# Weight sums of the gate/up quads: accumulating transfers for all of them, and five quads a block instead of four

## The chip, the core and the metric

The kernel runs on one core of a Trainium2 chip. A core has TensorE (PE: matrix products, with a separate weight load, PEld), VectorE (DVE), ScalarE (ACT), GpSimd (POOL) and SyncE (SP), each with an instruction queue of its own that it works off strictly in order, and sixteen DMA engines that serve the transfers of all queues. SyncE issues nearly all loads here; GpSimd issues the transfers that add what they bring to what already lies in on-chip memory (SBUF). The metric is the device time in microseconds (us), the median of several runs.

## The reference

A block of a language model for 256 tokens of width 2048, in float32: a gated feed-forward, a mixer, and a second feed-forward.

```python
def _swiglu(x, w_gate, w_up, w_down):
    return (jax.nn.silu(x @ w_gate) * (x @ w_up)) @ w_down

f = _swiglu(_rmsnorm(h, ln_ffn1_pre[l]), ffn1_gate[l], ffn1_up[l], ffn1_down[l])
h = h + MACARON_WEIGHT * _rmsnorm(f, ln_ffn1_post[l])
mx = _hybrid_mixer(_rmsnorm(h, ln_mix_pre[l]), w_in[l], ...)
h = h + _rmsnorm(mx, ln_mix_post[l])
f = _swiglu(_rmsnorm(h, ln_ffn2_pre[l]), ffn2_gate[l], ffn2_up[l], ffn2_down[l])
h = h + MACARON_WEIGHT * _rmsnorm(f, ln_ffn2_post[l])
```

w_gate and w_up are 2048 x 5632, w_down is 5632 x 2048. The mixer isn't touched by the change.

## The kernel before, in words

Tokens are two halves of 128 rows (h = 0, 1). Every float32 operand is split into a high part (a cast on ScalarE, `wH<-w`) and a low remainder (a subtraction on VectorE, `wL<-w,wH`), and each product is three matmuls (`mm3`): high by high, high by low, low by high. Weights come as tiles of 128 rows by 512 columns (256 KB); two of them side by side fill one buffer of 128x1024, and one split handles both.

**Stages.** The first feed-forward's gate/up part takes from the start to about 440 us, its down part to about 685 us, the mixer to about 1300 us, and the second feed-forward the rest. The gate/up part has eleven blocks of 512 gate columns (`f`) and 512 up columns (`l`). A block runs over 16 row tiles of the weights (k = 0 to 15), with four sums in PSUM: f0, f1, l0, l1, one per column group and token half.

**Pairs and quads.** An ordinary step (`pair`, L902) loads the two tiles of rows k and k+1 for one column group and multiplies both by both token halves. A *quad* (`Columns`, L874) takes a 2 x 2 set of tiles, rows k and k+1 by gate and up, and forms the eight products with seven, after Strassen and Winograd. So each quad saves one product of three matmuls, and pays with sums of weight tiles and sums of token tiles (`sums`, L706). With g(k) and u(k) for the gate and up tile of row k, the sums of weights are t1 = u(k) + g(k), t3 = g(k+1) + g(k), t2 = u(k) + t3 and t4 = u(k+1) + t2.

A gate/up quad has two steps. `early` (L928) runs during the block ahead: it loads the four tiles, makes the sums, splits u(k), t2, t1 and t3 and does four of the seven products. `late` (L947) runs in the block itself: it loads g(k+1) and u(k+1) once more, splits them and t4, and does the other three. `block_seq` (L1016) mixes the late steps and pairs of one block with the early steps of the next.

**How the sums are made before.** `four` (L908) has two ways. In most quads VectorE adds: t1 and t3 in one instruction of 128x1024, t2 and t4 in one of 128x512 each (L932, L936). In the quads of index 3 (`GATE_ACC`, L56) SyncE loads g(k) twice into the buffer of t1 and t3, and GpSimd issues two transfers with `accum_op=ALU.add` (L925), which add u(k) and g(k+1) from memory onto them. `GATE1` and `GATE2` (L49) give the number of quads in each of the eleven blocks. The down part has ten quads for each half of its columns (`quad`, L972), two of them (`DOWN_ACC`, L55) with accumulating transfers.

**What sets the order.** The operations aren't issued as the code writes them: `Plan.simulate` (L312) lets a small model of the engines run, with durations (`cost`, L231), a transfer rate (`RATE`), a landing time and an extra for accumulating transfers (`ADDING`), deadlines and buffer counts, and writes down each engine's queue in the order in which the model issued (`emit`, L503, where L525 issues every instruction; that is why the profile shows L525 everywhere). On the chip every queue keeps that order, whatever lands late. Buffers: five of 128x1024 for loaded weights (`w32`), five each for `wH` and `wL`, and 36 units of 128x1024 for all else. `KEPT` (L116) says how many of the eleven results of the gate/up part are split at once and written out for later sums; the others are kept unsplit until the down part needs them, and the down part's quads begin after them.

Of the kernel before, what the change touches and what calls it, by code (L numbers as in the profile page):

```python
# [12 lines left out]
F32 = mybir.dt.float32  # L13
# [34 lines left out]
EASE = 2.0  # L48
GATE1 = [0, 0, 3, 4, 4, 4, 4, 4, 4, 4, 4]  # L49
GATE2 = [0, 0, 3, 4, 4, 4, 4, 4, 4, 4, 4]  # L50
# [54 lines left out]
CARRY = 1200.0  # L105
ADDING = 3000.0
SWITCH = 100.0
# [7 lines left out]
LEND = 11  # L115
KEPT = 4  # L116
IN_ORDER = ("w32", "wH", "wL")


class Plan:  # L120
# [110 lines left out]
    def cost(s, o, name, w, r, k):  # L231
# [642 lines left out]
class Columns:  # L874

    def __init__(s, blk, wf, cf, wl, cl, at, KT, sm, quads, bank, apart=None):
        s.b, s.wf, s.cf, s.wl, s.cl, s.at, s.KT, s.sm = blk, wf, cf, wl, cl, at, KT, sm
        s.dma = ()
        s.quads, s.new, s.apart = quads, bank, apart
# [27 lines left out]

    def four(s, k):  # L908
        q = s.b
        t13 = q.unit((P, 2, 512), F32, "t13")  # L910
        if k not in s.dma:
            va, vb = q.raw4(k, s.wf, s.cf, s.wl, s.cl)
            q.nc.vector.tensor_tensor(out=t13, in0=va,
                                      in1=vb[:, :1].to_broadcast([P, 2, 512]), op=ALU.add)
            return va, vb, t13
        get = lambda k, f: (s.wf if f else s.wl)[k * P:k * P + P,
                                                 (s.cf if f else s.cl):][:, :512]
        for i in range(2):
            q.nc.sync.dma_start(out=t13[:, i], in_=get(k, 1))
        va, vb = [q.raw().rearrange("p (a c) -> p a c", a=2) for _ in range(2)]  # L920
        q.nc.sync.dma_start(out=va[:, 0], in_=get(k, 0))
        q.nc.sync.dma_start(out=va[:, 1], in_=get(k + 1, 1))
        q.nc.sync.dma_start(out=vb[:, 1], in_=get(k + 1, 0))
        for i in range(2):
            q.nc.gpsimd.dma_start(out=t13[:, i], in_=get(k + i, i), accum_op=ALU.add)  # L925
        return va, vb, t13
# [45 lines left out]
    def quad(s, k):  # L972
        q = s.b
        V = q.nc.vector
        va, vb, t13 = s.four(k)
        b11, b22 = q.halves(va)
        V.tensor_tensor(out=vb[:, 0], in0=va[:, 0], in1=t13[:, 1], op=ALU.add)
        t4 = q.tmp("t4")
        V.tensor_tensor(out=t4, in0=vb[:, 1], in1=vb[:, 0], op=ALU.add)
        t1, t3 = q.halves(t13)  # L980
        t2, b21 = q.halves(vb)
        h4 = q.unit((P, 2, 512), F32R, "h4")
        q.split(t4, h4[:, 0], h4[:, 1])
# [30 lines left out]
class Kernel(Block):  # L1014
# [30 lines left out]

    def ffn(s, wg, wu, wd, uT, rs, gpost, resid, emit, reload, quads, downs, xs=None):
        nc = s.nc
# [38 lines left out]
        for b in range(1, nb):  # L1086
            jobs[b] = Columns(s, wg, b * 512, wu, b * 512, s.T_at(nT) if b > 1 else at, NKD,
                              su, [2 * i for i in range(quads[b])],
                              s.psum if b % 2 else s.bank)
            jobs[b].dma = [2 * i for i in GATE_ACC if i < quads[b]]  # L1090
        for b in range(1, nb):
# [12 lines left out]
        s.down(wd, late_T, NKF, s.post(gpost, 0.5, resid, emit, reload, xs is None), raws,  # L1104
               downs, 4 * KEPT, DOWN_ACC)

# [30 lines left out]
    def down(s, wd, at, KT, ev, raws, plan, q0=0, acc=()):  # L1137
        sm = {}
        for c, (nq, first, step) in ((0, plan[0]), (2, plan[1])):
            J = Columns(s, wd, c * 512, wd, c * 512 + 512, at, KT, sm,  # L1140
                        [q0 + 2 * i for i in range(nq)], s.bank, s.psum)
            quads = list(J.quads)
            J.dma = [quads[i] for i in acc if i < nq]
            tail = J.rest[-min(TRAIL, KT - 2 * nq) // 2:] if c else []
# [863 lines left out]
def kernel(tc, x, ln_ffn1_pre, ln_ffn1_post, ffn1_gate, ffn1_up, ffn1_down,  # L2008
# [11 lines left out]
    with ExitStack() as ctx:  # L2020
# [10 lines left out]
        def at_tok(u):  # L2031
            return lambda h, c: u[h][c // 2][:, (c % 2) * 512:(c % 2) * 512 + 512]
# [68 lines left out]
        def emit1(h, c, ap):  # L2101
# [3 lines left out]
              at_tok(xr), emit1, load_to(xr, lambda h: x[0, h * P:h * P + P]),  # L2105
              GATE1, DOWN1, (load, turn, squares, finish, scaled))
        uT3, rs3, pre3, _ = s.next_pre(lambda: s.col["ln_ffn2_pre"])
# [9 lines left out]
        def emit(h, c, ap, queue=nc.sync):  # L2117
            queue.dma_start(out=out[0, h * P:h * P + P, c * 512:c * 512 + 512], in_=ap)
        s.ffn(ffn2_gate[0], ffn2_up[0], ffn2_down[0], uT3, rs3, ln_ffn2_post[0],
              at_tok(h2), emit, load_to(h2, lambda h: hsp[1, h]), GATE2, DOWN2)  # L2120
        s.plan.emit()
# [49 lines left out]
```

## Time and profile before

| | |
|---|---|
| time, median of 3 runs | 1985.75 us (1985.63 to 1986.48) |
| the profiled execution: its time | 1987.15 us |
| its span, first to last instruction | 1985.4 us |
| granted TensorE clock | 0.999 |
| busy PE, DVE, ACT, POOL | 1974.6, 1813.0, 1210.7, 118.8 us |
| moved by DMA | 503.19 MB, mean 253 GB/s |

A row of the profile's groups names the line, the engine, the operation, what it writes and reads, the shape, the count, then busy us and mean ns of one, and the idle time of the engine just before them with what ended it. Numbers are left off the names of buffers, so `w` is any buffer of loaded weights and `t` any unit for sums. A view by stretches gives each engine's busy time in a piece of the span and the share of the sixteen DMA engines. The view of the DMA queues gives for each queue packets, MB, and the time of its packets as a share of the time of sixteen engines: q1 is SyncE's queue, q0 GpSimd's. Matmuls overlap in the rows (389 ns each), so their pace is read from the time between them.

### The profile page before, as it was taken

The page shows a single profiled execution, that of the slowest core. Times are in us where ns is not written, and L with a number is a line of the kernel's source. Part 1 is how long each engine was busy: PE and PEld are TensorE (multiplying, and loading weights), DVE is VectorE, ACT ScalarE, POOL GpSimd, SP SyncE. Part 2 cuts the span into 40 slices and gives each one's busy share as a digit, 9 for nine tenths or more (in the row PEclk, how much of TensorE's full clock was granted, in tenths as well). Part 3 has the DMA queues.
Part 4 walks back from the last instruction along what each step waited for, and adds up shares of the span by engine and source line. Part 5 has one row for each costly group of instructions (what it writes and reads, how often), then busy time and mean ns, then how long its engine had stood idle before and what let it go on. Part 6 is the DMA issues. An engine that isn't in the chain of part 4 may idle for free.

```text
span 1985.4 us, 28410 instructions
## 1 busy us (share of the span) xinstructions
PE 1974.6 (99%) x9692; PEld 1630.8 (82%) x9692; DVE 1813.0 (91%) x2303; ACT 1210.7 (61%) x1552; POOL 118.8 (6%) x190
## 2 busy tenths in 40 slices
PE   9999999999999999999999999999999999999998
PEld 7888888888888888888888788888888888888886
DVE  7999999989998988998899779998999999899986
ACT  8566656666655767864665455665556556666553
POOL 0000000000001020001400100010000000000000
PEclk9999999999999999999999999999999999999999
DMA  9988899887768888757666498777898999777684
GB/s 319 323 266 283 276 317 312 278 257 228 242 198 274 261 259 277 216 167 252 178 194 190 128 322 262 240 258 241 273 307 293 317 287 286 255 230 236 204 287 144
DMA packets 278000, 503.19 MB, mean 253 GB/s; under 512 B 25056, under 2 KB 53472, under 8 KB 277856
## 3 DMA queue, kind: packets, MB, share of 16 engines
q1 hardware_dynamic: 267280, 478.96, 73.6%
q0 software_dynamic: 10144, 22.03, 5.3%
q8 instruction: 76, 1.25, 0.2%
q14 instruction: 68, 0.56, 0.1%
q10 hardware_dynamic: 432, 0.40, 0.1%
HBM read 473.11 MB, written 27.13 MB: 252 GB/s over the span
## 4 chain that ended last, share of the span: by engine, by line
PE 94%; DVE 3%; DMA 1%; ACT 1%; issue 1%; SPq 0%; POOLq 0%; ACTq 0%; DVEq 0%
PE l L525 33%; PE f L525 30%; PE mm L525 22%; PE p L525 6%; DVE wL L525 1%; DMA w<-in_ffn_gate_dram 1%; PE pY L525 0%; PE pA L525 0%; ACT wH L525 0%; PE tr L525 0%; PE pU L525 0%; DMA w<-in_ffn_down_dram 0%; DVE AR L525 0%; DMA w<-in_w_in_dram 0%; PE pSa L525 0%
## 5 line engine op out<-in xcount | busy, mean ns | idle before, releaser
L525 ACT CAST wH<-w 128x1024 fp32r<-128x1024 f32 (+1 forms) x712 | 727.4, 1042 | 508.4 <-PE f L525 105.1
L525 DVE TENSOR_TENSOR wL<-w,wH 128x1024 fp32r<-128x1024 f32 (+1 forms) x712 | 848.8, 1209 | 92.8 <-ACT wH L525 68.8
L525 PE MATMUL l<-wL,xH 128*128 128x512 f32 x828 | 322.3, 389 | 0.0
L525 PE MATMUL l<-wH,xL 128*128 128x512 f32 x828 | 322.2, 389 | 0.0
L525 PE MATMUL l<-wH,xH 128*128 128x512 f32 x828 | 322.1, 389 | 0.0
L525 PE MATMUL f<-wH,xH 128*128 128x512 f32 x608 | 236.6, 389 | 0.0
L525 PE MATMUL f<-wH,xL 128*128 128x512 f32 x608 | 236.6, 389 | 0.0
L525 PE MATMUL f<-wL,xH 128*128 128x512 f32 x608 | 236.5, 389 | 0.0
L525 PE MATMUL mm<-wL,xH 128*128 128x512 f32 (+1 forms) x568 | 220.2, 388 | 1.1 <-DVE wL L525 1.1
L525 PE MATMUL mm<-wH,xH 128*128 128x512 f32 (+1 forms) x568 | 220.8, 389 | 0.5 <-ACT xH L525 0.5
L525 PE MATMUL mm<-wH,xL 128*128 128x512 f32 (+1 forms) x568 | 219.1, 386 | 0.0
L525 ACT CAST wH<-t 128x1024 fp32r<-128x1024 f32 (+1 forms) x158 | 165.3, 1046 | 81.6 <-PE f L525 32.3
L525 DVE TENSOR_TENSOR wL<-t,wH 128x1024 fp32r<-128x1024 f32 (+1 forms) x158 | 191.5, 1212 | 17.0 <-ACT wH L525 7.9
L525 PEld LDWEIGHTS l<-wL,xH 128*128 128x128 f32 x828 | 155.4, 188 | 32.4 <-DVE wL L525 0.2
L525 PEld LDWEIGHTS l<-wH,xH 128*128 128x128 f32 x828 | 155.4, 188 | 32.3
L525 PEld LDWEIGHTS l<-wH,xL 128*128 128x128 f32 x828 | 155.4, 188 | 32.2
L525 DVE TENSOR_TENSOR t<-w,w 128x1024 f32<-128x1024 f32 (+1 forms) x170 | 167.2, 988 | 7.5 <-DMA w<-in_ffn_down_dram 5.6
L525 PEld LDWEIGHTS f<-wL,xH 128*128 128x128 f32 x608 | 114.1, 188 | 23.7
L525 PEld LDWEIGHTS f<-wH,xL 128*128 128x128 f32 x608 | 114.1, 188 | 23.7
L525 PEld LDWEIGHTS f<-wH,xH 128*128 128x128 f32 x608 | 114.1, 188 | 23.6
L525 PEld LDWEIGHTS mm<-wL,xH 128*128 128x128 f32 x568 | 106.8, 188 | 22.7 <-DVE wL L525 2.3
L525 PEld LDWEIGHTS mm<-wH,xH 128*128 128x128 f32 x568 | 106.7, 188 | 22.5 <-ACT xH L525 0.9
(320 smaller groups left out, 2861.3 us busy)
## 6 DMA issues: line engine op xcount, KB each, us to landing
w<-in_w_in_dram SPq DMA_DIRECT2D x120, 512.0 KB, 4.5
w<-in_ffn_up_dram SPq DMA_DIRECT2D x106, 512.0 KB, 5.1
w<-in_ffn_up_dram SPq DMA_DIRECT2D x210, 256.0 KB, 5.1
w<-in_ffn_gate_dram SPq DMA_DIRECT2D x102, 512.0 KB, 6.0
w<-in_ffn_gate_dram SPq DMA_DIRECT2D x202, 256.0 KB, 5.0
w<-in_ffn_down_dram SPq DMA_DIRECT2D x96, 512.0 KB, 4.8
w<-in_ffn_down_dram SPq DMA_DIRECT2D x152, 256.0 KB, 4.1
cx<-T SPq DMA_DIRECT2D x33, 512.0 KB, 3.8
```

The lines of the kernel that those rows point to most:

```text
L525: ins = o.fn(*[real(x) for x in o.a], **{n: real(x) for n, x in o.k.items()})
```

## The change

Each gate/up quad now has a *mode* (`GMODE1`: 3, 3, 3, 1, 1 for the five quads of a block). In mode 1, VectorE makes t1, t3 and t2 as before; t4 begins as a copy of t2 by ScalarE, onto which a transfer from GpSimd's queue adds u(k+1). In mode 3, moreover, two transfers add u(k) and g(k) onto the loaded g(k) and g(k+1), which makes t1 and t3 in place; VectorE then makes t2 alone. Mode 3 takes its second buffer from the units instead of the weight ring. Counted from 0, blocks 2 to 9 have five quads and block 10 has four, where block 2 had three and blocks 3 to 10 four; blocks 0 and 1 have none. The down part's quads all go by VectorE (`DMODE1` is zero). The planner's extra for an accumulating transfer falls from 3000 to 800 ns, and `KEPT` from 4 to 2.

```diff
-GATE1 = [0, 0, 3, 4, 4, 4, 4, 4, 4, 4, 4]
+GATE1 = [0, 0, 5, 5, 5, 5, 5, 5, 5, 5, 4]
...
-DOWN_ACC = 6, 8
-GATE_ACC = 3,
+GMODE1 = [[3, 3, 3, 1, 1]] * 11
+GMODE2 = GMODE1
+DMODE1 = [0] * 10, [0] * 10
...
-ADDING = 3000.0
+ADDING = 800.0
...
-KEPT = 4
+KEPT = 2
...
+            if "accum_op" in k:
+                o.pace = 1000.0
...
+    def load(s, out, k, f):
+        s.b.nc.sync.dma_start(out=out, in_=s.at_w(k, f))
+
+    def plus_w(s, out, k, f):
+        s.b.nc.gpsimd.dma_start(out=out, in_=s.at_w(k, f), accum_op=ALU.add)
...
     def early(s, k):
-        va, vb, t13 = s.four(k)
-        V.tensor_tensor(out=va[:, 1], in0=va[:, 0], in1=t13[:, 1], op=ALU.add)
...
+        mode = s.mode(i)
+        va, vb = [q.raw(mode & 2).rearrange("p (a c) -> p a c", a=2) for _ in range(2)]
+        s.load(va[:, 0], k, 0)
+        s.load(vb[:, 0], k, 1)
+        s.load(va[:, 1], k + 1, 1)
...
-        V.tensor_tensor(out=s.t4[i - i % 2][:, i % 2], in0=vb[:, 1], in1=va[:, 1],
-                        op=ALU.add)
-        b11, t2 = q.halves(va)
-        t1, t3 = q.halves(t13)
+        t4 = s.t4[i - i % 2][:, i % 2]
+        if mode & 2:
+            s.plus_w(vb[:, 0], k, 0)
+            s.plus_w(va[:, 1], k, 1)
+            t2 = vb[:, 1]
+            add(t2, va[:, 0], va[:, 1])
+        else:
+            if not mode & 1:
+                s.load(vb[:, 1], k + 1, 0)
+            t13 = q.unit((P, 2, 512), F32, "t13")
+            add(t13, va, vb[:, :1].to_broadcast([P, 2, 512]))
+            t2 = va[:, 1]
+            add(t2, va[:, 0], t13[:, 1])
+        if mode & 1:
+            q.nc.scalar.copy(t4, t2)
+            s.plus_w(t4, k + 1, 0)
```

**GpSimd's queue, first feed-forward.** Before, in the middle of the gate/up part (`t` is the buffer of t1 and t3, two rows a block):

```order
L525 DMA t_359_1403<-in_ffn_gate_dram 128x512
L525 DMA t_359_1403<-in_ffn_up_dram 128x512
L525 DMA t_441_1798<-in_ffn_gate_dram 128x512
L525 DMA t_441_1798<-in_ffn_up_dram 128x512
L525 DMA t_521_2133<-in_ffn_gate_dram 128x512
L525 DMA t_521_2133<-in_ffn_up_dram 128x512
```

These six rows stand for three blocks. Now, from one block's early steps (`w` are the buffers of loaded tiles in mode 3, `t` those of t4):

```order
L529 DMA w_404_1596<-in_ffn_gate_dram 128x512
L529 DMA w_405_1603<-in_ffn_up_dram 128x512
L529 DMA t_350_1593<-in_ffn_up_dram 128x512
L529 DMA t_406_1740<-in_ffn_up_dram 128x512
L529 DMA w_423_1672<-in_ffn_gate_dram 128x512
L529 DMA w_424_1680<-in_ffn_up_dram 128x512
L529 DMA w_432_1714<-in_ffn_gate_dram 128x512
L529 DMA w_433_1721<-in_ffn_up_dram 128x512
L529 DMA t_380_1833<-in_ffn_up_dram 128x512
L529 DMA t_406_1740<-in_ffn_up_dram 128x512
L529 DMA t_434_1943<-in_ffn_up_dram 128x512 x2
```

Three quads of mode 3 stand there with two rows each, and between them the transfers onto t4; in one queue they wait for loads, for ScalarE's copies and for each other's turn.

**SyncE's queue, the same places.** Before, a quad with accumulation (t_521) and one without (w_507, w_508):

```order
L525 DMA t_521_2133<-in_ffn_gate_dram 128x512
L525 DMA w_501_2141<-in_ffn_gate_dram 128x512
L525 DMA w_501_2141<-in_ffn_up_dram 128x512
L525 DMA w_507_2155<-in_ffn_up_dram 128x512
L525 DMA w_507_2155<-in_ffn_gate_dram 128x512
L525 DMA t_521_2133<-in_ffn_gate_dram 128x512
L525 DMA w_508_2175<-in_ffn_gate_dram 128x512
L525 DMA w_508_2175<-in_ffn_up_dram 128x512
```

Now, two quads of mode 3 (w_404 with w_405, w_423 with w_424) and one of mode 1 (w_378 with w_379); x<-cx brings back a block's result, turned:

```order
L529 DMA w_404_1596<-in_ffn_gate_dram 128x512
L529 DMA w_405_1603<-in_ffn_gate_dram 128x512
L529 DMA w_404_1596<-in_ffn_up_dram 128x512
L529 DMA w_375_1621<-in_ffn_gate_dram 128x2x512
L529 DMA x_315_1638<-cx_89 32x4x256 x4
L529 DMA w_378_1661<-in_ffn_up_dram 128x512
L529 DMA w_378_1661<-in_ffn_gate_dram 128x512
L529 DMA w_423_1672<-in_ffn_gate_dram 128x512
L529 DMA w_424_1680<-in_ffn_gate_dram 128x512
L529 DMA w_423_1672<-in_ffn_up_dram 128x512
L529 DMA w_379_1706<-in_ffn_gate_dram 128x512
```

Every quad has three loads in its early step now, where it had four or five; the rest of what it needs has moved to the queue above.

More of the change, by code (lines that the diff above doesn't have):

```diff
@@ L906, in pair, with at_w @@
                 s.mul(f"{b}{h}", s.rows(i, h), (wH, wL))
[L908 to L926, printed above, removed]
+    def at_w(s, k, f):
+        w, c = (s.wf, s.cf) if f else (s.wl, s.cl)
+        return w[k * P:k * P + P, c:c + 512]
+    def load(s, out, k, f):
+        s.b.nc.sync.dma_start(out=out, in_=s.at_w(k, f))
+    def plus_w(s, out, k, f):
+        s.b.nc.gpsimd.dma_start(out=out, in_=s.at_w(k, f), accum_op=ALU.add)
     def early(s, k):
@@ L974, in quad @@
         V = q.nc.vector
-        va, vb, t13 = s.four(k)
+        add = lambda o, x, y: V.tensor_tensor(out=o, in0=x, in1=y, op=ALU.add)
+        mode = s.mode(s.quads.index(k))
+        va, vb = [q.raw(x).rearrange("p (a c) -> p a c", a=2) for x in (False, mode & 1)]
+        t13 = q.unit((P, 2, 512), F32, "t13")
+        t4 = vb[:, 0] if mode & 1 else q.tmp("t4")
+        if mode & 2:
+            s.load(t13[:, 0], k, 1)
+            s.load(t13[:, 1], k, 1)
+        s.load(va[:, 0], k, 0)
+        if not mode & 2:
+            s.load(vb[:, 0], k, 1)
+        s.load(va[:, 1], k + 1, 1)
+        s.load(vb[:, 1], k + 1, 0)
+        if mode & 2:
+            for i in range(2):
+                s.plus_w(t13[:, i], k + i, i)
+        else:
+            add(t13, va, vb[:, :1].to_broadcast([P, 2, 512]))
         b11, b22 = q.halves(va)
-        V.tensor_tensor(out=vb[:, 0], in0=va[:, 0], in1=t13[:, 1], op=ALU.add)
-        t4 = q.tmp("t4")
-        V.tensor_tensor(out=t4, in0=vb[:, 1], in1=vb[:, 0], op=ALU.add)
+        add(vb[:, 0], va[:, 0], t13[:, 1])
+        if not mode & 1:
+            add(t4, vb[:, 1], vb[:, 0])
         t1, t3 = q.halves(t13)
         t2, b21 = q.halves(vb)
+        if mode & 1:
+            s.plus_w(t4, k + 1, 0)
         h4 = q.unit((P, 2, 512), F32R, "h4")
@@ L1089, in ffn @@
                               s.psum if b % 2 else s.bank)
-            jobs[b].dma = [2 * i for i in GATE_ACC if i < quads[b]]
+            jobs[b].mode = lambda i, b=b: modes[b][i]
         for b in range(1, nb):
@@ L1142, in down @@
             quads = list(J.quads)
[L1143 removed]
+            J.mode = lambda i, c=c: acc[c // 2][i] if acc else 0
             tail = J.rest[-min(TRAIL, KT - 2 * nq) // 2:] if c else []
```

26 lines of the change are left out of this document (20 added, 6 removed).

## The prediction

> **What bounds the kernel now.** I read the page first: engine shares, then the chain that ended last.
>
> ```profile
> span 1985.4 us, 28410 instructions
> PE 1974.6 (99%) x9692; PEld 1630.8 (82%) x9692; DVE 1813.0 (91%) x2303; ACT 1210.7 (61%) x1552; POOL 118.8 (6%) x190
> ...
> PE 94%; DVE 3%; DMA 1%; ACT 1%; issue 1%; SPq 0%; POOLq 0%; ACTq 0%; DVEq 0%
> ```
>
> TensorE (PE) is busy 99% of the span and is 94% of the chain; DMA is 1% of it. Then the chain in order of time, inside the first feed-forward's gate/up stage. Its columns are start, length, engine and group.
>
> ```profile
> 176.78 11.56 PE l L525 x51
> ...
> 217.58 11.56 PE l L525 x51
> ...
> 258.38 11.56 PE l L525 x51
> ```
>
> The same run of 51 matmuls returns every 40.80 us: that is one block of 512 gate and 512 up columns. One matmul costs 11.56 / 51 = 0.2267 us; a block has 16 x 2 x 2 x 3 = 192, less 3 for each of four quads, 180, and 180 x 0.2267 = 40.8 us. So PE runs without a hole, and nothing but fewer matmuls can shorten it as long as its food arrives. Who brings the food is the next view: busy time by stretches (PE, PEld, DVE, ACT, POOL, then granted clock, DMA share of 16 engines, GB/s). The first two are the stretches in which quads are made.
>
> ```profile
> 53.00:435.00 382.00, 382.00 (x1686) 316.28 (x1686) 363.95 (x383) 232.19 (x255) 14.94 (x19) 1.00 0.89 289
> 1342.00:1723.00 381.00, 381.00 (x1682) 315.48 (x1682) 355.98 (x369) 228.79 (x250) 13.97 (x16) 1.00 0.88 286
> 272.00:312.00 40.00, 40.00 (x178) 33.10 (x178) 38.46 (x41) 23.85 (x26) 1.79 (x2) 1.00 0.97 313
> 388.20:395.00 6.80, 6.80 (x32) 5.63 (x31) 6.07 (x8) 2.75 (x3) 0.00 (x0) 1.00 1.04 291
> ```
>
> PE is full, DVE (VectorE) at 95%, and the DMA engines at 0.89 and 0.88: a second resource stands just under its limit. One 40 us stretch reads 0.97, and 6.8 us around a pair of accumulating transfers read 1.04, so packets of the two queues overlap a little and the scale ends slightly above 1. Last, the DMA queues in the two stretches (packets, MB, share of 16 engines); q1 carries SyncE's loads, q0 GpSimd's transfers. First 53 to 435 us:
>
> ```profile
> q1 hardware_dynamic: 58233, 105.94, 82.4%
> q0 software_dynamic: 2304, 4.20, 6.8%
> q8 instruction: 13, 0.21, 0.2%
> q14 instruction: 12, 0.10, 0.1%
> ```
>
> And 1342 to 1723 us:
>
> ```profile
> q1 hardware_dynamic: 57391, 104.35, 81.0%
> q0 software_dynamic: 2304, 4.20, 6.9%
> q8 instruction: 14, 0.23, 0.2%
> q14 instruction: 12, 0.10, 0.1%
> ```
>
> This is the row that decides. In the first, q1 took 0.824 x 382 = 314.8 us of all sixteen engines for 105.94 MB, 2.97 us per MB, or **0.779 us** for a load of 128x512 (0.262 MB). q0's 4.20 MB are exactly sixteen accumulating transfers of that size: 0.068 x 382 = 26.0 us, **1.62 us** each. The second gives 0.775 and 0.069 x 381 / 16 = 1.64. A byte that is added on the way costs the DMA engines 2.1 times a byte that is only loaded. A closer look, 388 to 396 us, where the engines had work from both queues throughout:
>
> ```profile
> q1 hardware_dynamic: 918, 1.66, 62.7%
> q0 software_dynamic: 288, 0.52, 36.5%
> ```
>
> Two accumulating transfers took 0.365 x 8 = 2.92 us, 1.46 each, while the loads beside them paid 0.627 x 8 / 1.66 = 3.02 us per MB. So the doubled price isn't time in which the engines could have served others for free.
>
> **The change part by part.**
>
> *Matmuls.* Each feed-forward goes from 35 quads to 44: 9 x 3 = 27 matmuls fewer, 27 x 0.2267 = 6.1 us, 12.2 us in all. This is the whole gain that is to be had, since PE has no hole that could be closed: 382 becomes 375.9 us in the first stretch, 381 becomes 374.9 in the second.
>
> *Transfers.* Counted in loads of 128x512 per feed-forward. Before: blocks 0 and 1 take 32 each, block 2 (three quads) 5 pairs x 4 + 3 x 6 = 38, each of eight blocks with four quads 4 pairs x 4 + 3 x 6 + 7 = 41; 430 loads and 8 x 2 = 16 accumulations. After: a quad of mode 3 takes 3 loads, 3 accumulations and 2 later loads, one of mode 1 takes 3, 1 and 2. A block of five has 3 pairs x 4 + 5 x 5 = 37 loads and 3 x 3 + 2 = 11 accumulations; the last, with four, 36 and 10. Sum: 64 + 8 x 37 + 36 = 396 loads, 8 x 11 + 10 = 98 accumulations. So 34 loads go and 82 accumulations come. At the prices of the first stretch: -34 x 0.779 + 82 x 1.62 = -26.5 + 132.8 = +106.3 us of all sixteen engines. They had 82.4 + 6.8 + 0.2 + 0.1 = 89.5% of 382 = 341.9 us of work; now 448.2 us. In the second: -26.4 + 134.5 = +108.1 on 88.2% of 381 = 336.0; now 444.1 us. PE needs 375.9 and 374.9. **The DMA engines become the bound.** How long a stretch lasts is its work divided by the share they reach. Both queues will hold work in most of a block (11 x 1.62 of some 48 us is q0's), so I take 1.02, between the 1.04 of the busy 6.8 us and the 0.97 of the busiest block: 448.2 / 1.02 = 439.4 and 444.1 / 1.02 = 435.4, that is +57.4 and +54.4 us. The matmul gain is inside: it is what PE no longer waits for, not a term of its own.
>
> Bounds: with 0.97, 462.1 and 457.8, +157 us together. With 1.11, which is more than any row shows, 403.8 and 400.1, +41 us.
>
> *DVE.* The rows (shape, count, busy, mean ns of one):
>
> ```profile
> L525 DVE TENSOR_TENSOR wL<-w,wH 128x1024 fp32r<-128x1024 f32 x694 | 834.9, 1220 | 86.2 <-ACT wH L525 62.3 <-issue 9.7 <-PE l L525 4.4
> L525 DVE TENSOR_TENSOR t<-w,w 128x1024 f32<-128x1024 f32 x96 | 117.1, 1220 | 5.6 <-DMA w<-in_ffn_down_dram 5.6
> L525 DVE TENSOR_TENSOR w<-w,t 128x512 f32<-128x512 f32 x120 | 82.4, 686 | 0.8
> L525 DVE TENSOR_TENSOR sf<-x 128x256 f32<-128x256 f32 x24 | 9.1, 421 | 0.0
> ```
>
> Gate/up sums per feed-forward: before 27 x 1.22 + 70 x 0.686 = 81.0 us, after (17 quads of mode 1 with the wide add, 44 narrow adds) 17 x 1.22 + 44 x 0.686 = 50.9: 30 us less. Nine more quads bring 1.5 more splits each, 9 x 1.5 x 1.22 = 16.5, and a third call of the row sums 4 x 0.421 + 1.22 = 2.9. Net 11 us less on DVE. PE has no hole there that DVE made, so this buys nothing; the down stage gets four wide adds back and two moved splits, 6 x 1.22 = 7.3 us per feed-forward:
>
> ```profile
> 440.00:685.00 245.00, 244.47 (x1080) 201.99 (x1079) 226.75 (x258) 149.75 (x169) 11.83 (x36) 1.00 0.75 241
> 1745.00:1985.00 240.00, 234.09 (x1028) 192.51 (x1027) 210.68 (x240) 132.40 (x152) 8.01 (x10) 0.99 0.69 219
> ```
>
> DVE idles 18 and 29 us there: free, and at most 7 us each where the idle time lies in the wrong place. The 8 accumulations and 4 loads that the down stage loses change nothing at a DMA share of 0.75.
>
> *ScalarE and GpSimd.* 44 copies of 128x512 per feed-forward are new.
>
> ```profile
> L525 ACT CAST h<-t 128x512 fp32r<-128x512 f32 x46 | 28.4, 618 | 22.9 <-DVE t L525 22.9
> ...
> L525 ACT COPY s<-f 128x512 f32<-128x512 f32 x19 | 11.3, 593 | 0.9 <-DVE f L525 0.9
> ```
>
> The nearest rows give 0.6 us: 26 us on an engine with 382 - 232 = 150 us free, cover enough. GpSimd's instructions for 98 transfers:
>
> ```profile
> L525 POOL DMA_DIRECT2D t<-in_ffn_up_dram x8 | 8.8, 1098 | 5.9 <-DMA t<-in_ffn_gate_dram 5.9
> L525 POOL DMA_DIRECT2D t<-in_ffn_gate_dram x8 | 7.2, 900 | 329.3 <-DMA t<-in_ffn_gate_dram 78.3 <-DVE t L525 73.3 <-DMA w<-in_ffn_gate_dram 71.1
> ```
>
> 98 x 1.0 = 98 us of 382: no bound by itself.
>
> *New waits.* GpSimd's queue now holds the chain of a quad: its first two accumulations wait for loads, the third for ScalarE's copy, which waits for VectorE's add, which waits for the second accumulation. Behind a late one stand the accumulations of the next quad; behind the add on VectorE the splits of ordinary pairs, and behind these PE. Before, such waits cost next to nothing in 53 to 435 us (total us, times, longest):
>
> ```profile
> ACT wH L525 <- DMA w<-in_ffn_up_dram: 3.1, 4, 1.7
> ACT wH L525 <- DMA w<-in_ffn_gate_dram: 2.8, 3, 2.2
> ```
>
> The fourth sum isn't used until a later step, so its landing is covered. I put no extra term on this; it is the third rival.
>
> Sum: 1985.75 + 57.4 + 54.4 = 2097.6, say **2098 us**. The profiled execution took 1987.15 us for a span of 1985.4, the median is 1985.75; the growth is simply added to the median.
>
> **The rivals.** *A, on the other side: the accumulations hide, PE stays the bound.* 1985.75 - 12.2 = 1973.5 us. It needs the engines to do 448.2 us of work in 375.9: a share of 1.19, or packets 16% quicker than the mean of this stage. For it: loads alone run faster at times, as the GB/s in 40 slices of 53 to 435 us show.
>
> ```profile
> GB/s 408 229 300 292 343 266 359 323 174 223 212 279 273 320 299 283 371 349 128 264 358 396 155 260 352 404 243 275 264 363 363 249 203 307 357 279 258 258 393 131
> ```
>
> 408 against a mean of 289. Against it: no row reads over 1.04, and where accumulations ran at that share the rate was 291, not 400. It decides from an accumulation's price of (375.9 - (341.9 - 26.0 - 26.5)) / 98 = 0.88 us downwards.
>
> [...]
>
> *B: hardly over the edge.* Share 1.11 to 1.16 under a constant backlog: 403.8 and 400.1 down to 386.4 and 382.8 us, 2027 down to 1992 us. For it: the 1.04 was reached with only two accumulations in flight.
>
> *C: the chains of waits starve the DMA engines too.* VectorE stands at a late sum, buffers come free late, SyncE can't issue, and the share falls to 0.92: 487.2 and 482.7, +105 and +102, 2193 us. For it: the engines' queues are fixed in advance with shorter landing times (800 ns for an addition, not 3000). Against it: today's 0.97 block with buffers as tight.
>
> That the change doesn't do what it says is no rival: the instruction order holds 196 accumulations and 54 matmuls fewer.
>
> **How the numbers follow.** Forecast 0.66; A 0.08, with 0.02 for a draw at the edge where A and B meet; B 0.10; C 0.14. The range is the share from 1.11 (2027) to 0.94 (476.8 and 472.4, +186, so 2172, rounded to 2175); A, B and C lie outside it, and with them a third of the chance, less the near half of C's spread and of B's, which reach into it: about 0.2 is left out. A measurement of this kernel tells about 0.2%, 4 us, from no change. Faster 0.08 (A), same 0.02, slower 0.90.
>
> **What would show it.** Right: over the two stages a DMA share near 1, q0 near 98 x 1.62 / 439 = 36%, PE with holes that end at VectorE or ScalarE and behind these at DMA, a block period of 46 to 48 us, and down stages and mixer as long as before. Wrong: a period of 39.9 us with PE full (A, and then q0's price per MB must have fallen); a share well below 0.95 with long waits of GpSimd or VectorE for landings (C); growth outside the two stages.

## The result, and the profile after

The changed kernel takes 2011.0 us (2008.4 to 2013.24), the kernel before on the same chip 1985.92 us (1985.63 to 1986.48): a ratio of 1.0126, 95% interval 1.0108 to 1.0143. The forecast was 2098 us, in a range of 2027 to 2175. It is slower, as forecast, but by 25 us and not by 112. The profiled execution took 2013.24 us, 26.1 us more than that of before. The page after:

```profile
span 2011.5 us, 28759 instructions
...
PE 1979.7 (98%) x9638; PEld 1624.6 (81%) x9638; DVE 1801.3 (90%) x2283; ACT 1280.7 (64%) x1676; POOL 255.8 (13%) x338
...
PE 73%; DMA 14%; DVE 7%; issue 2%; ACT 2%; SPq 0%; DVEq 0%; POOLq 0%; ACTq 0%
```

54 matmuls are gone, and yet the span is longer. In the chain PE fell from 94% to 73%, DMA rose from 1% to 14%: the end is now set by matmuls that stand behind transfers. Where the time lies is read from the stretches. The stretch of 53 to 435 us before holds blocks 1 to 9 (block 10 ends at 463 us, not at the 440 given above). Before, the first feed-forward's block 1 and the eight blocks behind it (PE, PEld, DVE, ACT, POOL, clock, DMA share, GB/s):

```profile
53.00:106.00 53.00, 53.00 (x235) 43.85 (x235) 52.84 (x59) 28.46 (x32) 2.49 (x5) 1.00 0.92 305
106.00:435.00 329.00, 329.00 (x1453) 272.42 (x1452) 311.10 (x325) 203.73 (x223) 12.44 (x14) 1.00 0.89 287
```

After, the same pieces, then both together, the stretch behind them and the second feed-forward's gate/up stage:

```profile
53.00:117.00 64.00, 61.91 (x266) 50.78 (x266) 57.93 (x65) 40.64 (x48) 14.51 (x19) 0.97 0.98 275
117.00:451.00 334.00, 324.49 (x1401) 265.11 (x1400) 294.62 (x303) 222.71 (x266) 68.31 (x78) 0.98 1.06 319
53.00:451.00 398.00, 386.40 (x1665) 315.88 (x1665) 352.56 (x367) 263.35 (x314) 82.82 (x97) 0.98 1.05 312
451.00:700.00 249.00, 249.00 (x1106) 206.18 (x1106) 239.22 (x273) 156.50 (x184) 5.66 (x29) 1.00 0.69 222
1358.00:1751.00 393.00, 384.38 (x1663) 311.13 (x1663) 341.38 (x349) 261.62 (x310) 80.35 (x94) 1.00 1.05 311
```

The two gate/up stages grew by 398 - 382 = 16 us and 393 - 381 = 12 us; behind them PE is full again. Block 1 is 11 us longer (64 against 53), but 31 more matmuls are done in it, mostly of later blocks, which are 7.0 us at 0.2267 us each: it lost 4 us. Behind it 52 matmuls fewer take 5 us more, so most of the loss, some 17 us, lies there. In both stages PE has holes (11.6 and 8.6 us), VectorE and ScalarE are further from full than PE, and the DMA share went from 0.89 and 0.88 to 1.05. The queues from 53 to 451 us:

```profile
q1 hardware_dynamic: 54485, 98.71, 69.6%
q0 software_dynamic: 13824, 25.17, 35.0%
```

And from 1358 to 1751 us:

```profile
q1 hardware_dynamic: 53655, 97.17, 69.8%
q0 software_dynamic: 13479, 24.65, 34.7%
```

GpSimd's queue takes 35% of all sixteen engines, where it took 6.8%. What a backlog does to a load shows in the time from its issue to its landing (the last column). Before:

```profile
w<-in_ffn_gate_dram SPq DMA_DIRECT2D x202, 256.0 KB, 5.0
```

After, for the same load and for the transfers onto t4:

```profile
w<-in_ffn_gate_dram SPq DMA_DIRECT2D x272, 256.0 KB, 8.0
...
t<-in_ffn_up_dram POOLq DMA_DIRECT2D x88, 256.0 KB, 7.2
```

5.0 us became 8.0. The waits of 53 to 451 us (us in total, times, longest):

```profile
POOL t L529 <- ACT t L529: 151.7, 25, 17.6
POOL w L529 <- DMA w<-in_ffn_gate_dram: 77.4, 17, 13.4
ACT wH L529 <- DVE w L529: 33.8, 8, 10.2
ACT t L529 <- DVE w L529: 31.9, 18, 6.9
...
ACT wH L529 <- DMA w<-in_ffn_up_dram: 16.3, 10, 3.2
DVE t L529 <- DMA w<-in_ffn_gate_dram: 15.7, 6, 4.5
...
DVE w L529 <- DMA w<-in_ffn_gate_dram: 1.0, 1, 1.0
```

Most links of the chain that the prediction described stand there: GpSimd waits for loads and for ScalarE's copy, the copy for VectorE's sum, the wide sum and the casts for late loads. The link of mode 3, VectorE's narrow sum behind an accumulation, hardly does: that sum waited for a transfer once, 1.0 us. One hole of PE, on VectorE's queue:

```profile
265.83 1.23 DVE L529 TENSOR_TENSOR t<-w,w 128x1024 f32<-128x1024 f32 x1 [4.49 <-DMA w<-in_ffn_gate_dram]
...
268.93 1.23 DVE L529 TENSOR_TENSOR wL<-w,wH 128x1024 fp32r<-128x1024 f32 x1 [1.15 <-ACT wH L529]
```

And on PE's:

```profile
268.95 0.50 PE L529 MATMUL l<-wH,xH 128*128 128x512 f32 x1 [1.74 <-ACT wH L529]
270.21 0.79 PE L529 MATMUL l<-wL,xH 128*128 128x512 f32 x1 [0.76 <-DVE wL L529]
```

A wide sum stood 4.49 us for a late load; the narrow sum, the cast and the split of the same quad came late behind it, and PE waited 1.74 us for the cast and 0.76 for the split. The chain of the profile leads on from that load to a block's result that is read back (`x<-cx`, 7.40 us) and written out before (`cx<-T`, 7.82 us): SyncE's transfers stand in such chains as well.

### The profile page after: what moved, and what is told of

The parts are those of the page before. It is cut to its first block, busy times and chain, and to the rows that moved or that the text cites. A ratio compares the mean times of both kernels' runs of the same rounds, so it can differ in the third digit from the quotient of the medians.

```text
span 2011.5 us, 28759 instructions
## 1 busy us (share of the span) xinstructions
PE 1979.7 (98%) x9638; PEld 1624.6 (81%) x9638; DVE 1801.3 (90%) x2283; ACT 1280.7 (64%) x1676; POOL 255.8 (13%) x338
## 2 busy tenths in 40 slices
DMA packets 288948, 522.10 MB, mean 260 GB/s; under 512 B 26784, under 2 KB 55200, under 8 KB 288800
## 4 chain that ended last, share of the span: by engine, by line
PE 73%; DMA 14%; DVE 7%; issue 2%; ACT 2%; SPq 0%; DVEq 0%; POOLq 0%; ACTq 0%
PE l L529 24%; PE mm L529 20%; PE f L529 20%; DMA w<-in_ffn_gate_dram 8%; PE p L529 6%; DVE wL L529 4%; DMA w<-in_ffn_up_dram 3%; DMA x<-cx 1%; ACT wH L529 1%; DMA cx<-T 1%; DMA w<-in_w_in_dram 1%; DVE w L529 0%; PE pY L529 0%; DVE sg L529 0%; PE pA L529 0%
## 5 line engine op out<-in xcount | busy, mean ns | idle before, releaser
L529 ACT CAST wH<-w 128x1024 fp32r<-128x1024 f32 (+1 forms) x766 | 782.7, 1043 | 463.7 <-PE mm L529 90.4
L529 DVE TENSOR_TENSOR wL<-w,wH 128x1024 fp32r<-128x1024 f32 (+1 forms) x766 | 911.9, 1211 | 112.1 <-ACT wH L529 106.3
L529 PE MATMUL f<-wH,xH 128*128 128x512 f32 x536 | 210.1, 392 | 0.4 <-DVE f L529 0.4
L529 PE MATMUL f<-wH,xL 128*128 128x512 f32 x536 | 209.6, 391 | 0.0
L529 DVE TENSOR_TENSOR wL<-t,wH 128x1024 fp32r<-128x1024 f32 (+1 forms) x138 | 159.9, 1158 | 4.2 <-ACT wH L529 2.7
L529 ACT CAST wH<-t 128x1024 fp32r<-128x1024 f32 (+1 forms) x138 | 138.1, 1001 | 37.7 <-DVE t L529 16.9
L529 PE MATMUL f<-wL,sH 128*128 128x512 f32 x322 | 127.5, 396 | 4.1 <-DVE wL L529 4.0
L529 DVE TENSOR_TENSOR t<-w,w 128x1024 f32<-128x1024 f32 (+1 forms) x88 | 105.5, 1199 | 28.5 <-DMA w<-in_ffn_gate_dram 23.7
L529 PE MATMUL f<-wH,sH 128*128 128x512 f32 x322 | 127.1, 395 | 3.0 <-DVE sg L529 2.8
L529 PE MATMUL f<-wH,sL 128*128 128x512 f32 x322 | 126.5, 393 | 0.0
```

Of the source, the lines that this page charges most:

```text
L529: ins = o.fn(*[real(x) for x in o.a], **{n: real(x) for n, x in o.k.items()})
```

## The experiments

Two theories. **Theory 1:** a gate/up stage is as long as the larger of two works, PE's and that of the DMA engines, the latter at prices under a backlog and a share near 1.05. **Theory 2:** the stage is as long as the chain of waits through queues whose order is fixed, GpSimd's above all; which engine has how much work matters little. "Before" is 1986.0 to 1986.5 us beside all of them.

### Is it the price of adding?

*e1_plain* is the kernel after, but its transfers on GpSimd's queue load without adding (the sums of weights are then wrong); order, counts, bytes and waits stay.

```diff
-ins = o.fn(*[real(x) for x in o.a], **{n: real(x) for n, x in o.k.items()})
+ins = o.fn(*[real(x) for x in o.a], **{n: real(x) for n, x in o.k.items()
+                                       if n != "accum_op"})
```

> The changed kernel with every instruction in the same order and with the same waits, but the 196 accumulating transfers don't add: they only load (the sums are wrong). Theory 1, work of the DMA engines: with the changed kernel's own prices (0.736 us a load, 1.45 an accumulation) a stage's work falls from 417 to 417 - 96 x 0.71 = 349 us, under PE's 376, so the growth goes and the matmul gain shows: 1974 to 1988 us. Theory 2, the chain of waits in fixed queues (load, GpSimd, VectorE, ScalarE, GpSimd): every wait still stands there, so most of the growth stays: 2000 to 2011 us.

*e2_extra* is the kernel before with a load of 512 KB in each ordinary gate/up step, which nobody reads; each takes one of the 36 units, and the planner writes new queues around them (the matmuls keep their order, VectorE's and ScalarE's work does not).

```diff
+        if s.KT == NKD:
+            s.b.get_w(w, k, 2, c0, 512, own=True)
```

> The kernel before, with its sums as they were, and beside each of the 90 ordinary pair steps per feed-forward from block 1 on one more load of 512 KB into a unit that nobody reads. It adds work for the DMA engines and no chain. Theory 1: a stage's work at the loaded prices is 297 + 23 + 1 = 321, and 170 loads of 0.736 in the stage make it 446; divided by the share of 1.05 that is 425 us against PE's 382, twice 43 more: some 2070 us, and a share of 1.05 in the stages. Theory 2: nobody waits for these loads, so 1986 to 2000 us.

Measured: e1 1978.28 us (1976.61 to 1979.56), 0.9957 [0.9943, 0.9972], 33 us below the kernel after and faster than before. Its stretch of 53 to 435 us and its two queues there:

```profile
53.00:435.00 382.00, 379.60 (x1667) 313.50 (x1666) 353.54 (x365) 263.35 (x314) 50.03 (x95) 1.00 0.93 324
```
```profile
q1 hardware_dynamic: 54402, 98.56, 74.7%
q0 software_dynamic: 7634, 24.98, 18.4%
```

The same 25 MB in the same order cost 18.4% of 382 us, 95.3 transfers at 0.738 us; with adding they cost 1.45. PE is full but for 2.4 us. So the waits of the new order, as long as the transfers are cheap, cost almost nothing, though GpSimd still waits for ScalarE's copies (232.5 us from 53 to 440 us, after 151.7 from 53 to 451): theory 2 falls as an explanation of the whole. e1 makes more than the engines' work smaller: the transfers onto t4 land in 5.2 us instead of 7.2, and GpSimd is busy 0.53 us with one of its instructions in the stage instead of 0.85 (50.03 us for 95, 82.82 for 97). It shows that adding is what costs, and doesn't part the engines' work from the longer landing.

e2 took 2097.21 us (2091.29 to 2100.98), 1.0552 [1.053, 1.0574]: loads that no engine waits for lengthen the kernel by 111 us, more than expected. What the units and the new queues have in this isn't separated.

```profile
53.00:451.00 398.00, 369.94 (x1548) 292.04 (x1547) 331.16 (x339) 201.82 (x226) 12.64 (x14) 0.98 0.97 341
```

With nearly all work in SyncE's queue the share is 0.97; over this stretch shares above 1 were read only in kernels whose q0 took 28% or more (e3 1.01 at 0.299 x 382 / 398 = 28.7%, e10 0.97 at 23.7%). Theory 1 had put in 446 us of work at 1.05, 425 us a stage; the first stage, to the same count of matmuls, lasted 441 us (53 to 494), with 429 us of work at 0.97. Both were counted too high, and the share weighed more.

### How many transfers may add?

*e3_33111*, *e4_11111* and *e5_five_old* change the modes of the five quads: two of mode 3; none (only t4 by a transfer); and VectorE's sums for all but the quad of index 3, which keeps two accumulations as before, though now in place (mode 2).

```diff
-GMODE1 = [[3, 3, 3, 1, 1]] * 11
+GMODE1 = [[3, 3, 1, 1, 1]] * 11   # e3
+GMODE1 = [[1, 1, 1, 1, 1]] * 11   # e4
+GMODE1 = [[0, 0, 0, 2, 0]] * 11   # e5
```

*e6_four_acc* keeps the modes and takes back the fifth quad: GATE1 and GATE2 are `[0, 0, 3, 4, 4, 4, 4, 4, 4, 4, 4]` again.

> The changed kernel with modes 3, 3, 1, 1, 1 for a block's quads instead of 3, 3, 3, 1, 1: 18 accumulations fewer per feed-forward, 9 wide adds more on VectorE. Theory 1: work 417 - 18 x 1.45 = 391, at 1.05 373 us, just under PE's 376; VectorE 353 + 9 x 1.22 = 364. PE becomes the bound again or nearly: 1976 to 1992 us. Theory 2: GpSimd's chain shrinks from 11 to 9 transfers a block, so about a fifth of the 25 us goes: some 2006 us.

> The changed kernel with mode 1 for all quads: 54 accumulations fewer per feed-forward, 27 wide adds more on VectorE. Theory 1: DMA work 417 - 54 x 1.45 = 339 us, out of the way, but VectorE gets 353 + 27 x 1.22 = 386 us of work in a stage of which PE needs 376, so it becomes the bound: 386 to 396 us a stage, 1990 to 2010 us in all, slower than with 3, 3, 1, 1, 1. Theory 2: five transfers a block instead of 11, no chain of two before VectorE's add: faster than 3, 3, 1, 1, 1.

> Five quads a block with the sums as before (VectorE, and two accumulating transfers in the quad of index 3), planner constants and buffers of the changed kernel. Theory 1 (each engine's work against PE's): DMA 44 quads of 6 loads and 18 accumulations, out of the way; VectorE gets 364 + 16.5 (splits) + 2.9 (row sums) + about 9 x 2.6 (sums of nine more quads) = 406 us against PE's 376: some 410 us a stage, 2035 to 2055 us in all. If so, the accumulations are what makes five quads bearable and not what spoils them. Theory 2 (the accumulations' waits are the cost): about 1974 to 1990 us.

> Four quads a block as before, with modes 3, 3, 3, 1. Theory 1: 89 accumulations and 387 loads per feed-forward, work 417 - 9 x (0.74 + 1.45) = 398, at 1.05 379 us, just under PE's 382: 1986 to 1996 us; no gain over before, since PE had no hole. Theory 2: ten transfers in the chain of a block instead of 11: 2005 to 2011 us.

| kernel | us | ratio to before |
|---|---|---|
| e3_33111 | 1994.34 (1992.06 to 1997.75) | 1.0040 [1.0025, 1.0055] |
| e4_11111 | 1986.55 (1985.41 to 1989.06) | 1.0003 [0.9993, 1.0012] |
| e5_five_old | 2006.65 (2006.17 to 2008.28) | 1.0104 [1.0089, 1.0119] |
| e6_four_acc | 1988.03 (1986.79 to 1989.87) | 1.0010 [1.0001, 1.0020] |

Their stretches, e3:

```profile
53.00:435.00 382.00, 376.72 (x1646) 307.70 (x1645) 354.64 (x367) 259.34 (x311) 67.22 (x79) 1.00 1.03 309
```

e4:

```profile
53.00:435.00 382.00, 377.49 (x1654) 310.95 (x1653) 375.03 (x385) 260.99 (x313) 39.50 (x47) 1.00 0.92 287
```

e5:

```profile
53.00:451.00 398.00, 386.30 (x1674) 314.25 (x1673) 396.66 (x430) 240.49 (x272) 16.59 (x21) 0.99 0.88 289
```

e6:

```profile
53.00:117.00 64.00, 64.00 (x284) 53.01 (x283) 55.71 (x59) 40.60 (x48) 15.39 (x20) 1.00 1.08 331
...
53.00:451.00 398.00, 398.00 (x1757) 329.56 (x1756) 335.33 (x339) 259.40 (x299) 76.77 (x90) 1.00 1.02 309
```

Each stage names its bound. With old sums VectorE is full (396.66 of 398) while DMA is at 0.88; with only t4 by transfers VectorE is at 98% and PE short of full by 4.5 us; with two quads of mode 3 DMA is at 1.03. With four quads, all accumulated, PE is full although DMA stands at 1.02, and at 1.08 in block 1: little room is left, but none was needed. Theory 1 gave the right bound for e4, e5 and e6. For e3 it had PE full or nearly, and PE fell short by 5.3 us beside a share of 1.03. Its sizes were off three times: e3 a little slower than its range and e4 faster, so that their order is the rival's, and e5 far cheaper than its 2035 us or more. Why VectorE's extra work was counted too high there stays open.

### The planner's numbers

*e7_plan_old* puts back both numbers that the change gave the planner, *e11_adding_old* and *e12_kept_old* one of them each.

```diff
-ADDING = 800.0
+ADDING = 3000.0   # e7, e11
-KEPT = 2
+KEPT = 4          # e7, e12
```

> The changed kernel with the planner's extra for an accumulating transfer at 3000 ns again and KEPT at 4: the queues' order allows longer landing times, the work is the same. Theory 1: the DMA engines' work sets the time, 2003 to 2015 us. Rival (the order expects landings too early): with a landing of 7 to 9 us allowed for, the waits of VectorE and ScalarE shrink and the time falls below 2000 us.

> The changed kernel with only the planner's extra for an accumulating transfer at 3000 ns again (KEPT stays 2). If this constant is what made the version with both old constants 16 us slower, 2020 to 2030 us; if KEPT was, 2008 to 2014 us.

> The changed kernel with only KEPT at 4 again (the extra stays 800 ns). The other half of the same question: 2008 to 2014 us if the extra was the cause, 2020 to 2030 us if KEPT was.

e7 2027.65 us (2024.47 to 2030.55), 1.0208 [1.0193, 1.0223]; e11 2008.05 us (2004.4 to 2009.95), 1.0107 [1.0093, 1.0121]; e12 2032.98 us (2029.72 to 2035.39), 1.0234 [1.022, 1.0248]. The extra for accumulations is worth nothing that can be told from the kernel after; `KEPT` is worth 22 us. e7 lies outside what either theory gave: theory 1 had at most 2015 us, the rival less than 2000. e12:

```profile
53.00:451.00 398.00, 377.78 (x1609) 305.63 (x1608) 341.76 (x350) 255.69 (x304) 81.98 (x96) 0.97 1.03 300
```

The work is the same, but the share is 1.03 and PE's holes add up to 20 us. A result that is split at once holds two units of 128x1024 where an unsplit one holds one, so `KEPT` 4 takes two units away for most of the stage. Whether it is these units was tried by taking one away, and by freeing one and two more; no instruction comes or goes, but the planner writes new queues each time.

```diff
-NUNITS = 36
+NUNITS = 35   # e14
-KEPT = 2
+KEPT = 1      # e15
+KEPT = 0      # e16
```

> The kernel after with 35 units of 128x1024 instead of 36; every transfer, sum and matmul stays. If the loss with KEPT 4 (22 us for two results that are held as two split units instead of one unsplit) is a lack of units for transfers that could have been issued, one unit less costs some 8 to 14 us: 2018 to 2026 us, with a DMA share of 1.03 to 1.04 in 53 to 451 us. If it is something else about KEPT (the split at once in blocks 3 and 4, or the earlier begin of the down part's sums): 2008 to 2014 us.

> The kernel after with KEPT 1: one result fewer is split at once, so one unit more is free from block 2 on. Lack of units: 5 to 10 us faster than after, 2001 to 2006 us, with fewer holes of PE. Something else: 2008 to 2014 us, or slower where the down part has to split later.

> The kernel after with KEPT 0: no result is split at once, two units more are free. Lack of units: 8 to 16 us faster than after in the two gate/up stages, 1995 to 2003 us if the down stages stay as long; theory 1 puts a floor under it, the work of the DMA engines at their best share, 417.5 / 1.08 = 387 us for the first stage, 11 us less than now. Something else: 2008 us or more.

e14 2030.6 us (2026.0 to 2031.04), 1.0217 [1.0202, 1.0232]; e15 2018.5 us (2017.65 to 2021.57), 1.0164 [1.0149, 1.0179]; e16 2013.22 us (2008.31 to 2013.46), 1.0129 [1.0114, 1.0144]. One unit less costs 20 us, more than the 8 to 14 expected. SyncE's waits for VectorE's sums that are made in loaded tiles, over the whole run, after:

```profile
SPq L529 <- DVE w L529: 44.9, 33, 3.2
```

and in e14:

```profile
SPq L529 <- DVE w L529: 81.7, 41, 10.7
```

The issuing of loads stands longer, at worst 10.7 us instead of 3.2. But in e12, which the units were to explain, this wait is as it was in the kernel after:

```profile
SPq L529 <- DVE w L529: 43.4, 29, 3.4
```

And units given back bring nothing: e16 is like the kernel after, e15 7 us slower. Of these orders e14's is the furthest from that of the kernel after on VectorE and ScalarE, and e13 below loses 12 us with all its units, by a new order alone. So the units are not shown to be the cause, neither of e12's 22 us nor of e14's 20; 36 with `KEPT` 2 is not short of them, since more bring nothing.

### Block 1

Block 1 has a hole of PE of 2.1 us, and VectorE has a third call of the token sums there. *e13_sums_late* puts that call off, by an addition to its due time; the queues are planned anew around it. (Its expectation counts block 1 as 10 of the 16 us; without the matmuls that moved into it, it is 4.)

```diff
-                s.sums(x.rearrange("p (a b) (h t) -> p a b h t", a=2, h=2), su)
+                with s.set(lag=s.nc.lag if i < 2 else 60000.0):
+                    s.sums(x.rearrange("p (a b) (h t) -> p a b h t", a=2, h=2), su)
```

> The kernel after, unchanged but for the third call of the token sums, which is put off behind the other work of VectorE in the first block. Theory 1 (the DMA engines' work sets the two stages): the work stays, and the DMA engines have no backlog to work off in block 1, so what that block lost (10 us of the 16 us by which the first stage grew) is partly given back: 2000 to 2006 us, the block of 53 to 117 us 56 to 60 us long. Rival (the first block is long because its transfers are late, not because of VectorE): 2008 to 2014 us, block as long as before.

2022.63 us (2019.36 to 2025.86), 1.0181 [1.0164, 1.0198]: both theories missed, by 8.6 us and more. The stretches:

```profile
53.00:117.00 64.00, 64.00 (x284) 52.99 (x284) 57.54 (x64) 43.27 (x50) 14.46 (x19) 1.00 1.04 296
117.00:451.00 334.00, 320.00 (x1378) 258.81 (x1377) 291.80 (x301) 221.18 (x264) 68.35 (x78) 0.99 1.05 315
```

The hole in block 1 is gone: PE is full to 117 us and has done 284 matmuls instead of 266. Behind it PE does 1378 instead of 1401 at the same DMA share, and over the whole stretch both kernels stand equal, 1660 and 1665 (the trace may lack a few). So closing the hole of block 1 won nothing in this stage: the time won on VectorE early is given back later in it, as one expects where the DMA engines are the bound. The total rose in the second feed-forward instead: from its first silu (`sg<-f`) to its last it takes 1380.9 to 1775.7 us, 394.8, against 1379.6 to 1765.9, 386.3, in the kernel after. That is the same work in another order.

### A version that beats both

If three engines stand near their limits, the sums should be shared among them: one quad of mode 3 a block, four of mode 1. *e8_mix* takes this with three quads in block 2 (four in the second feed-forward), *e9_mix_b2* makes those of block 2 three of mode 3 in both, and *e10_mix_late* adds to e9 the edit of e13.

```diff
-GATE1 = [0, 0, 5, 5, 5, 5, 5, 5, 5, 5, 4]
+GATE1 = [0, 0, 3, 5, 5, 5, 5, 5, 5, 5, 4]   # e8, e9, e10
-GATE2 = [0, 0, 5, 5, 5, 5, 5, 5, 5, 5, 4]
+GATE2 = [0, 0, 4, 5, 5, 5, 5, 5, 5, 5, 4]   # e8; e9 and e10 with 3
-GMODE1 = [[3, 3, 3, 1, 1]] * 11
+GMODE1 = [[3, 1, 1, 1, 1]] * 11                   # e8
+GMODE1 = [[3, 3, 3]] * 3 + [[3, 1, 1, 1, 1]] * 8  # e9, e10
```

> Modes 3, 1, 1, 1, 1, and fewer quads where the run begins: 3 in block 2 of the first feed-forward and 4 in the second's. Theory 1: DMA work 417 - 36 x 1.45 = 365 us, at 1.05 348; VectorE 353 + 18 x 1.22 = 375; PE about 377: all three near their limit, 1978 to 1986 us, so at best a little faster than before. Theory 2: between modes 3, 3, 1, 1, 1 and 1, 1, 1, 1, 1, 1988 to 1992 us.

> As the mix of modes 3, 1, 1, 1, 1, but block 2 has three quads, all of mode 3, in both feed-forwards. In the first feed-forward's block 1 VectorE was busy 61 of 64 us and PE had a hole of 4.6 us. Theory (VectorE's work in block 1 makes that hole): two wide adds of 1.22 us less there, the hole shrinks by 2 to 5 us: 1979 to 1983 us. Rival (the hole comes from elsewhere, or the run is at its floor): 1983 to 1986 us.

> The same with the third call of the token sums, which only the fifth quad from block 3 on needs, given a later due time, so that its 2.9 us of VectorE move out of the chain of sums at 52 to 71 us. Theory: 1 to 3 us below the kernel that it is made from, 1977 to 1981 us. Rival: the same time.

e8 1984.03 us (1982.41 to 1986.92), 0.9990 [0.9980, 0.9999]; e9 1984.36 us (1982.47 to 1989.36), 0.9992 [0.9983, 1.0001]; e10 **1981.12 us** (1979.11 to 1982.44), 0.9972 [0.9961, 0.9983], faster than before and than after. e9's time is its rival's: PE's hole in block 1 shrank from 4.6 us (e8) to 1.6, and the kernel got no faster. e10:

```profile
53.00:117.00 64.00, 64.00 (x284) 53.01 (x283) 61.01 (x69) 41.86 (x49) 11.66 (x16) 1.00 1.05 325
...
53.00:451.00 398.00, 396.90 (x1749) 327.73 (x1748) 378.28 (x392) 274.60 (x324) 54.96 (x65) 1.00 0.97 298
1358.00:1740.00 382.00, 382.00 (x1686) 316.12 (x1686) 358.32 (x367) 264.42 (x313) 47.43 (x55) 1.00 0.95 293
```

PE is full to 1.1 us, DMA at 0.97 and VectorE at 95%. Here, where the DMA engines keep some slack, e10 with the late call of the sums is 3 us below e9 (the two intervals just touch); beside the kernel after the same edit cost 12 us. Both come with new queues, so what the call itself is worth isn't shown. 42 matmuls fewer than before are 9.5 us, of which 5.1 arrive.

## Why the prediction was right in direction and wrong in size

**The bound: right.** "The DMA engines become the bound": share 1.05, q0 at 35% where 36% was named, PE with holes behind VectorE, ScalarE and transfers, down stages and mixer as before. e1 shows that the price of adding does it.

**The work: too high, and this is the first step that failed** ("At the prices of the first stretch"). From the rows after: q1 0.696 x 398 = 277.0 us for 98.71 MB, 0.736 us a load; q0 0.350 x 398 = 139.3 us for 25.17 MB, 96 transfers, **1.45 us** each; with 0.3% for the rest 417.5 us. The forecast had 448.2: 11 us too much for loads (16 by the price of 0.779, less 5 for more bytes than it counted), 16 us too much for accumulations at 1.62, and 3 us for two that lie outside the stretch. The prices were means of a stage in which the engines had slack. In fuller stretches both came out lower, if not in step with the share: a load cost 0.779 us at a share of 0.89 (before), 0.759 at 0.93 (e1), 0.726 at 0.97 (e2), 0.736 at 1.05 (after); an accumulation 0.071 x 398 / 18 = 1.57 at 0.88 (e5), 0.174 x 382 / 44 = 1.51 at 0.92 (e4), 1.45 after and 0.319 x 398 / 87 = 1.46 in e6:

```profile
q0 software_dynamic: 12528, 22.81, 31.9%
```

Why a packet is quicker then, no run shows. The better price for accumulations lay in the prediction itself: the view of 388 to 396 us, where both queues had work, gave 1.46, and the stretch inside it 1.04 (for a load it gave 3.02 us per MB, 0.79, no better than the mean). It was used to confirm the 1.62, not to replace it. With 1.46 for all 98 accumulations and 1.04 the stages come out at 314.8 - 26.5 + 98 x 1.46 + 1.2 = 432.6, by 1.04 416, and 308.6 - 26.4 + 143.1 + 1.1 = 426.4, by 1.04 410: 2049 us, and more than half of the error is gone.

**The share: too low, the second step that failed** ("I take 1.02"). At 1.02 the measured work gives 409 us, at 1.05 the 398 that came. So of the 41 us by which the first stage was overestimated 30 are the work and 11 the share; the second stage is alike (412 us of work done in 393).

**The lower bound** failed with them: 2027 us was the old work at a share of 1.11. No stage reached 1.11; cheaper packets did what the bound allowed only to the share. That is also why rival B's numbers hold the result by luck: B's condition, a share from 1.11 up, did not come.

**Rival A** wanted an accumulation under 0.88 us. e1 makes it 0.74, and A comes: 1978.28 us with PE full but for 2.4 us of the first stage, where A's sum, 12.2 us off before, said 1973.5. That fits the threshold, without showing where exactly it lies; the real price, 1.45, is above it. What adding costs is measured with it: after and e1 move the same 25 MB by the same queue for 139.3 and 0.184 x 382 = 70.3 us, near enough twice.

**Rival C** (share 0.92) did not come in the kernel after; but the order of the queues costs time. "I put no extra term on this" was too short: eight orders of the same work lie up to 25 us apart (below). All eight are slower than before by 21 us or more, so the order is not what made the kernel slower. What the waits cost in the kernel after itself is only bounded: nothing if 1.05 is the best that the engines do over a stage, 398 - 417.5 / 1.08 = 11 us if they could keep the 1.08 of e6's block 1 throughout, and 398 - 417.5 / 1.10 = 18 us a stage with the 1.10 that stretches of 3.4 us read (below).

**VectorE, ScalarE, GpSimd: right.** ScalarE's new copies measured 0.62 us for 0.6:

```profile
L529 ACT COPY t<-w 128x512 f32<-128x512 f32 x88 | 54.2, 621 | 66.3 <-DVE w L529 65.9 <-DVE wL L529 0.3
```

VectorE's relief bought nothing that shows, putting off the third call of the sums won nothing (e13), and the first down stage's longer sums lie beside a PE that is full (249.00 of 249).

**The block period** (46 to 48 us) was wrong with the rest: eight blocks from 117 to 451 us are 41.8 us each, against 329 / 8 = 41.1 before, and each of them lost some 2 us against PE's pace. Block 1 lost 4 us; the sum did not treat it apart.

## What to carry to other kernels

Take the price of a transfer from a stretch in which the queues it will share are backlogged, not from the mean of a stage with slack, and use the same stretch's share of the engines: here the two errors together made 25 us into 112. When work is moved from one engine near its limit to another near its limit, look for the mixture: with five quads a block and nearly all sums by VectorE it was 2007 us, with three quads of five in mode 3 2011, with one 1984 (e8) and 1981 (e10). And a hole that one sees at a bound stage's start need not be a cost: removed (e13), it came back later in the stage. Where a planner writes the queues, an edit changes the order of everything: here orders of the same work differ by up to 25 us, so a difference of that size between two plans has to be shown by more than one order.

## What was not expected of the hardware

**The clock halves after short holes, on a fixed grid.** Pairs of neighbouring stretches of 3.41 us in the kernel after (the count behind PE's busy time is of matmuls; the third-last column is the granted clock):

```profile
68.49:71.90 3.41, 1.32 (x6) 0.81 (x5) 3.41 (x4) 1.05 (x1) 0.00 (x0) 1.00 0.94 251
71.90:75.31 3.41, 3.41 (x10) 2.67 (x9) 3.41 (x5) 1.24 (x2) 0.00 (x0) 0.50 0.65 195
177.71:181.13 3.42, 2.13 (x10) 1.43 (x8) 0.99 (x1) 0.00 (x0) 1.47 (x2) 1.00 1.07 326
181.13:184.54 3.41, 1.99 (x9) 1.65 (x10) 2.25 (x4) 1.36 (x2) 0.98 (x2) 1.00 1.10 285
266.46:269.87 3.41, 1.25 (x5) 0.48 (x3) 2.22 (x3) 2.02 (x3) 0.00 (x0) 1.00 1.10 279
269.87:273.29 3.42, 3.08 (x7) 2.48 (x8) 2.63 (x4) 1.97 (x2) 0.00 (x0) 0.50 1.07 305
1498.67:1502.09 3.42, 1.62 (x8) 1.08 (x7) 3.39 (x5) 1.98 (x3) 0.86 (x1) 1.00 1.06 404
1502.09:1505.50 3.41, 3.41 (x10) 2.64 (x9) 3.41 (x4) 1.75 (x2) 0.00 (x0) 0.50 1.07 326
```

A stretch with 5, 6 or 8 matmuls, where a full one shows 16 or 17, is followed by one at half the clock; those with 9 and 10 are not (184.54 to 187.95 us reads 1.00 again). The slow stretches start at 71.90, 269.87, 314.27 (two in a row) and 1502.09 us, 58, 13 and 348 times 3.413 us apart; one more ends the kernel. How much work PE had in a stretch of the grid tells the two kinds apart in the traces of after and before, from 4 us on: the six stretches at full clock that half the clock followed had 1.12 to 1.62 us of it (two to six matmuls began in them), and no other had less than 1.99 us (seven or more began). In the slow stretches a matmul follows the other after 0.43 us, where it is 0.2267 at full clock:

```profile
271.23 0.63 PE L529 MATMUL f<-wH,sH 128*128 128x512 f32 x1
271.66 0.63 PE L529 MATMUL f<-wL,sH 128*128 128x512 f32 x1
272.08 0.63 PE L529 MATMUL f<-wH,sL 128*128 128x512 f32 x1
```

So a hole of some 2 us, if it falls into one stretch of the grid, costs, as an estimate from these rows, up to 3.41 / 2 = 1.7 us more for each slow stretch behind it.

**The same work in eight orders takes 2008 to 2033 us.** e7 and e11 to e16 have the 9638 matmuls, 2283 VectorE and 1676 ScalarE instructions of the kernel after, and its 522.10 MB to 0.01; only numbers that the planner goes by differ, and with them the order.

| kernel | us | mean granted clock of the profiled run |
|---|---|---|
| e11_adding_old | 2008.05 | 0.997 |
| after | 2011.0 | 0.995 |
| e16_kept0 | 2013.22 | 0.996 |
| e15_kept1 | 2018.5 | 0.993 |
| e13_sums_late | 2022.63 | 0.994 |
| e7_plan_old | 2027.65 | 0.992 |
| e14_units35 | 2030.6 | 0.992 |
| e12_kept_old | 2032.98 | 0.989 |

The clock falls with the time, by and large: 0.997 to 0.989 is 0.008 x 2020 = 16 us of full clock, of 25 us between the first and the last. That holes bring slow stretches is in the rows above; that these then cost all of the 16 us is not shown, since the DMA engines go on working in some of them (1.07) and not in others (0.65). Which property of an order makes the holes stays open.
